# First weights ahead of the tokens, half-column token loads, idle transposes, and layer norm squares about the first half's mean

## The chip, the cores and the metric

The kernel runs on one core of one Trainium2 chip. The metric is the device time of one execution in microseconds (us), smaller being better; a kernel's time is the median of several runs. TensorE (PE) multiplies, VectorE (DVE), ScalarE (ACT) and GpSimd (POOL) do the elementwise work, and SyncE (SP) issues the transfers (DMA).

## The reference

A two-layer encoder trunk on 512 tokens of width 1024, all in float32. Each layer is three sub-layers, and each ends in a layer norm of a scaled residual plus the sub-layer's output:

```
def layer_norm(x, g, b):
    mu = jnp.mean(xf, axis=-1, keepdims=True)
    var = jnp.mean(jnp.square(xf - mu), axis=-1, keepdims=True)
    y = (xf - mu) * lax.rsqrt(var + LN_EPS)
    return y * g + b

def swiglu(x, w_gate, w_up, w_down):
    return (jax.nn.silu(x @ w_gate) * (x @ w_up)) @ w_down
...
x = layer_norm(ALPHA * x + 0.5 * swiglu(x, ...), ...)
x = layer_norm(ALPHA * x + mix, ...)      # attention and S5 in layer 0, pooling and gMLP in layer 1
x = layer_norm(ALPHA * x + 0.5 * swiglu(x, ...), ...)
```

So there are six layer norms, four feed-forward blocks (FFN, inner width 2816) and two mixers.

## The kernel before

Tokens lie in four tiles of 128 rows. For the matmuls, x is held transposed: `xh` and `xl` are [128, 8 blocks of columns, 512 tokens]. Every float32 product is three matmuls of reduced-precision parts: `split` (lines 88 to 96) copies the high part on ACT (line 91) and subtracts it on DVE for the low part (line 93), and `mm3` (lines 120 to 126) issues hi x hi, hi x lo, lo x hi. Weights come as 512 KB blocks `raw` (four buffers), are split into `whi` and `wlo`, and are used once. `to_xt` (line 128) turns one token tile: for each half `h` of its columns, four PE transposes into one PSUM bank, then a split into `xh` and `xl`; so a tile gives two xh copies on ACT and two xl subtractions on DVE.

The start: `load_x` (line 207) asks on SP's queue, in turn, for token tile 0, gate weights 0, tile 1, gate weights 1, tiles 2 and 3. Tiles 0 and 1 are turned and gate weights split in a fixed order on ACT and DVE (`as_written` chains the instructions of a block on an engine). Tiles 2 and 3 are left in `pending`. The first FFN (`ffn`, line 222) takes the weights in groups of 256 columns, gate (`m` = 0) and up (`m` = 1). The first group is worked in two halves of tokens: 48 matmuls of 256 tokens for the gate, then `flush`, which runs what is pending, 48 for the up weights, then the other 256 tokens of both. `cols` (line 201) runs over the eight column blocks `k`. Beside these matmuls DVE does `s5_prepare` (line 509), some hundreds of small instructions that make the S5 mixer's tables from one packed input, `s5pk`; it lies in the buffer of tiles 0 and 1, so its load waits until they are turned. On PE the order is the order of the code; on DVE and ACT the scheduler sets it, outside the blocks that `as_written` chains.

The layer norm: each of six blocks ends in `ln_tile` (line 153) or in the same steps, per token tile: two `add_to` on DVE add a bank of 512 columns to the residual `z` and give its sum, `ln_rest` (line 165) makes the negative mean `nmu`, ACT squares both halves about it and sums them (line 173), DVE makes (z - mean) g (line 176), POOL adds the two sums (line 177) and makes the reciprocal deviation `rs` in two steps (`rstd`, lines 142, 143), and DVE scales (line 185, or 182 for the last FFN, whose halves go out by DMA). The next `flush` turns the tile for the next block.

Of the kernel before, what the change touches and what calls it, by code (L numbers as in the profile page):

```python
# [16 lines left out]
P = 128  # L17
# [16 lines left out]
LATE = 3  # L34
NEG = -1e30
# [13 lines left out]
class Trunk:  # L49
# [3 lines left out]
    def __init__(self, ctx, tc):  # L53
# [14 lines left out]
        self.pending = []  # L68
# [4 lines left out]
    @contextmanager  # L73
    def as_written(self, *engines):

        ins = self.nc.cur_bb.bb.instructions
        last = ins[-1]
        yield
        start = next(k for k in reversed(range(len(ins))) if ins[k] is last) + 1
        info = mybir.DependencyInfo(mybir.DependencyClass.NoSync, mybir.DependencyReason.DATA)  # L80
        for e in engines:
            todo = [i for i in ins[start:] if i.engine == e]
            for a, b in zip(todo, todo[1:]):
                self.tc.add_manual_dep(b, a.name, info, reason="as_written")
# [22 lines left out]

    def halves(self, raw, shape):
        hi = self.w.tile([P] + shape, F32R, tag="whi", name="whi")
        lo = self.w.tile([P] + shape, F32R, tag="wlo", name="wlo")  # L110
# [17 lines left out]
    def to_xt(self, t, src):  # L128
        for h in range(2):
# [23 lines left out]
    def ln_tile(self, t, z, p0, p1, yscale, g, b, out=None, spill=None):  # L153

        s = self.sm.tile([P, 6], F32, name="st")
# [9 lines left out]
    def ln_rest(self, t, z, s, junk, g, b, out=None, spill=None):  # L165


        nc = self.nc
        nmu = s[:, 2:3]
        nc.vector.scalar_tensor_tensor(out=nmu, in0=s[:, 0:1], scalar=s[:, 1:2], in1=self.cst[:, 1:2],  # L170
                                       op0=ALU.add, op1=ALU.mult)
        for h, p in enumerate(junk):
            nc.scalar.activation(out=p, in_=z[:, h * 512:(h + 1) * 512], func=AF.Square, bias=nmu,  # L173
                                 accum_out=s[:, 3 + h:4 + h])
        n = self.w.tile([P, D], F32, tag="zf", name="zf", bufs=2)
        nc.vector.scalar_tensor_tensor(out=n, in0=z, scalar=nmu, in1=g, op0=ALU.add, op1=ALU.mult)
        nc.gpsimd.tensor_tensor(out=s[:, 5:6], in0=s[:, 3:4], in1=s[:, 4:5], op=ALU.add)  # L177
        rs = self.rstd(s[:, 5:6], 1.0 / D, EPS)
# [22 lines left out]
    def cols(self, bks, stat, a=0, b=SEQ):  # L201

        for k in range(NK):
            for bk, f in bks:
# [3 lines left out]
    def load_x(self, x, xt):  # L208

        raw = []  # L210
        for t in range(NT):
            self.nc.sync.dma_start(xt[t], x[t * P:(t + 1) * P])
            if t < 2:
                raw.append(self.fetch(*self.coming[t]))
        with self.as_written(mybir.EngineType.Activation, mybir.EngineType.DVE):
            for t in range(2):
                self.to_xt(t, xt[t])
                self.got.append(self.halves(raw[t], self.coming[t][1]))
# [4 lines left out]
    def ffn(self, xt, wg, wu, wd, g_ap, b_ap, out=None, spill=None, fetch=None, side=None, res=4):  # L223
        nc, tc = self.nc, self.tc
        with tc.tile_pool(name="act", bufs=1, reuse_waits="tile") as ap, \
# [5 lines left out]
            with self.as_written(*([mybir.EngineType.PE] if late else [])):  # L231
                for fg in range(NF // 2):
# [19 lines left out]
                    if jobs:  # L252
                        for m in range(2):
                            self.cols(*jobs[m], 0, 256)
                            self.flush(0 if late else 1 - m)
# [1021 lines left out]
def kernel(ctx, tc, x, ln_g, ln_b, wg, wu, wd, ab_in, ab_out, rel, s5pk, w_glu,  # L1277
# [8 lines left out]
    with tc.tile_pool(name="xa", bufs=1, reuse_waits="tile") as xa:  # L1286
# [13 lines left out]
        first(wg[0, 0], 0, 256)  # L1300
        k.load_x(x, x_tiles())
# [62 lines left out]
```

## Time and profile before

| | |
|---|---|
| median of 3 runs | 1817.14 us (1815.19 to 1817.96) |
| the profiled execution | 1817.25 us, its span 1815.5 us |
| PE busy | 1786.5 us (98%), 8752 matmuls and transposes |
| DVE, ACT, POOL busy | 1104.4 (61%), 690.4 (38%), 32.1 us (2%) |
| DMA | 212.77 MB, 117 GB/s on average |
| mean granted PE clock | 0.998 |

The span runs from the first to the last instruction; the execution's time holds 1.75 us more. A row of a timeline gives start, length, engine, line, operation, output and inputs, and, in brackets, how long the engine stood idle before it and what ended that. Matmuls are pipelined, so the distance of two starts tells their cost, not the length of one.

### The profile page before, as it was taken

The page shows a single profiled execution, that of the slowest core. Times are in us where ns is not written, and L with a number is a line of the kernel's source. Part 1 is how long each engine was busy: PE and PEld are TensorE (multiplying, and loading weights), DVE is VectorE, ACT ScalarE, POOL GpSimd, SP SyncE. Part 2 cuts the span into 40 slices and gives each one's busy share as a digit, 9 for nine tenths or more (in the row PEclk, how much of TensorE's full clock was granted, in tenths as well). Part 3 has the DMA queues.
Part 4 walks back from the last instruction along what each step waited for, and adds up shares of the span by engine and source line. Part 5 has one row for each costly group of instructions (what it writes and reads, how often), then busy time and mean ns, then how long its engine had stood idle before and what let it go on. Part 6 is the DMA issues. An engine that isn't in the chain of part 4 may idle for free.

```text
span 1815.5 us, 22309 instructions
## 1 busy us (share of the span) xinstructions
PE 1786.5 (98%) x8752; PEld 1497.6 (82%) x8752; DVE 1104.4 (61%) x1783; ACT 690.4 (38%) x983; POOL 32.1 (2%) x119
## 2 busy tenths in 40 slices
PE   8999999999999999999999999999999999999998
PEld 7888888888887888888888888888878898888886
DVE  7866542266766657658436585574488566747635
ACT  4233431245767433333324333332264343333322
POOL 0000000010000100000000000000010000000000
PEclk9999999999999999999999999999999999999999
DMA  6335633255422551532334324223333152531321
GB/s 207 107 116 168 203 105 104 94 163 166 128 94 73 177 194 47 177 102 67 112 99 139 107 89 142 82 81 116 117 98 105 58 186 68 153 104 58 123 97 58
DMA packets 168377, 212.77 MB, mean 117 GB/s; under 512 B 7888, under 2 KB 130000, under 8 KB 168272
## 3 DMA queue, kind: packets, MB, share of 16 engines
q1 hardware_dynamic: 168272, 211.35, 37.0%
q8 instruction: 68, 1.11, 0.3%
q14 instruction: 37, 0.30, 0.1%
HBM read 196.12 MB, written 14.16 MB: 116 GB/s over the span
## 4 chain that ended last, share of the span: by engine, by line
issue 60%; PE 33%; DVE 3%; ACT 1%; DMA 1%; POOL 1%; POOLq 0%; SPq 0%; DVEq 0%; ACTq 0%
PE ps L124 10%; PE ps L125 10%; PE ps L126 10%; PE ps L810 1%; DVE wlo L93 1%; POOL rs L143 1%; DMA s5tl<-side 1%; PE ps L858 0%; PE ps L850 0%; PE ps L133 0%; DMA x<-in_x_dram 0%; DVE pl L93 0%; PE ps L849 0%; ACT ps L173 0%; POOL st L177 0%
## 5 line engine op out<-in xcount | busy, mean ns | idle before, releaser
L124 PE MATMUL ps<-xh,whi 128*128 128x512 f32 (+1 forms) x1696 | 639.0, 377 | 0.8 <-ACT xh L91 0.8
L125 PE MATMUL ps<-xl,whi 128*128 128x512 f32 (+1 forms) x1696 | 635.0, 374 | 4.0 <-DVE xl L93 4.0
L126 PE MATMUL ps<-xh,wlo 128*128 128x512 f32 (+1 forms) x1696 | 634.4, 374 | 0.0
L93 DVE TENSOR_TENSOR wlo<-raw,whi 128x1024 fp32r<-128x1024 f32 x313 | 381.7, 1221 | 337.5 <-ACT whi L91 334.9
L91 ACT ACTIVATE whi<-raw 128x1024 fp32r<-128x1024 f32 x313 | 330.3, 1058 | 655.1 <-PE ps L125 370.3
L124 PEld LDWEIGHTS ps<-xh,whi 128*128 128x128 f32 x1696 | 320.6, 189 | 59.8 <-issue 3.1
L125 PEld LDWEIGHTS ps<-xl,whi 128*128 128x128 f32 x1696 | 320.6, 189 | 59.4 <-DVE xl L93 5.2
L126 PEld LDWEIGHTS ps<-xh,wlo 128*128 128x128 f32 x1696 | 320.5, 189 | 56.7
L124 PE MATMUL ps<-whi,sl 128*128 128x512 f32 x480 | 187.2, 390 | 0.0
L126 PE MATMUL ps<-whi,sl 128*128 128x512 f32 x480 | 186.9, 389 | 0.0
L125 PE MATMUL ps<-wlo,sl 128*128 128x512 f32 x480 | 186.9, 389 | 0.0
L126 PEld LDWEIGHTS ps<-whi,sl 128*128 128x128 f32 x480 | 90.2, 188 | 18.7
L125 PEld LDWEIGHTS ps<-wlo,sl 128*128 128x128 f32 x480 | 90.2, 188 | 18.5
L124 PEld LDWEIGHTS ps<-whi,sl 128*128 128x128 f32 x480 | 90.2, 188 | 18.4
L162 DVE SCALAR_TENSOR_TENSOR xb<-ps,xb 128x512 f32<-128x512 f32 x128 | 83.0, 683 | 23.5 <-PE ps L126 23.4
L334 DVE SCALAR_TENSOR_TENSOR th<-th,ps 128x512 f32<-128x512 f32 x66 | 44.9, 684 | 73.5 <-ACT th L333 73.0
L333 ACT ACTIVATE th<-ps 128x512 f32<-128x512 f32 x66 | 38.8, 592 | 121.4 <-PE ps L126 121.4
L93 DVE TENSOR_TENSOR sl<-hb,sl 128x1792 fp32r<-128x1792 f32 x24 | 48.6, 2023 | 31.9 <-ACT sl L91 31.9
L341 DVE TENSOR_TENSOR hb<-th,ps 128x512 f32<-128x512 f32 x48 | 32.6, 687 | 56.0 <-PE ps L126 56.0
L91 ACT ACTIVATE sl<-hb 128x1792 fp32r<-128x1792 f32 x24 | 40.8, 1700 | 44.6 <-DVE hb L348 44.6
L91 ACT ACTIVATE whi<-b 128x1024 fp32r<-128x1024 f32 x36 | 38.1, 1059 | 39.6 <-PE ps L126 38.2
L93 DVE TENSOR_TENSOR wlo<-b,whi 128x1024 fp32r<-128x1024 f32 x36 | 44.0, 1221 | 14.2 <-ACT whi L91 14.2
(327 smaller groups left out, 1905.2 us busy)
## 6 DMA issues: line engine op xcount, KB each, us to landing
raw<-in_wg_dram SPq DMA_DIRECT2D x88, 512.0 KB, 3.6
raw<-in_wu_dram SPq DMA_DIRECT2D x88, 512.0 KB, 3.6
raw<-in_wd_dram SPq DMA_DIRECT2D x76, 512.0 KB, 3.3
b<-in_wd_dram SPq DMA_DIRECT2D x24, 512.0 KB, 5.4
raw<-in_ab_in_dram SPq DMA_DIRECT2D x20, 512.0 KB, 4.4
raw<-in_cd_in_dram SPq DMA_DIRECT2D x12, 512.0 KB, 3.7
x<-in_x_dram SPq DMA_DIRECT2D x8, 512.0 KB, 7.1
s<-zf SPq DMA_DIRECT2D x8, 512.0 KB, 4.5
```

The source lines that it names most:

```text
L91: nc.scalar.activation(out=hi, in_=src, func=AF.Copy, scale=scale)
L93: nc.vector.tensor_tensor(out=lo, in0=src, in1=hi.bitcast(F32), op=ALU.subtract)
L124: mm(ps, ah, bh, start=start, stop=False)
L125: mm(ps, ah, bl, start=False, stop=False)
L126: mm(ps, al, bh, start=False, stop=stop)
L143: nc.gpsimd.tensor_tensor(out=v[:, 1:2], in0=v[:, 0:1], in1=self.cst[:, 0:1], op=ALU.pow)
L162: self.nc.vector.scalar_tensor_tensor(out=zz, in0=p, scalar=scale, in1=zz, op0=ALU.mult, op1=ALU.add, **({} if total is None else {"accum_ ...
L333: nc.scalar.activation(out=th, in_=bk[0, f], func=AF.Tanh, scale=0.5)
L334: nc.vector.scalar_tensor_tensor(out=th, in0=th, scalar=1.0, in1=bk[0, f], op0=ALU.add, op1=ALU.mult)
L341: tt(out=hb[:, 0::7] if f == 0 else hb[:, 1:3], in0=th.rearrange("p (a c) -> p a c", a=2), in1=bk[1, f].rearrange("p (a c) -> p a c", a=2) ...
L810: nc.tensor.matmul(banks[h][:, o:o + w], a[r, i * P:i * P + P], b[r, :w], start=n == 0, stop=n == 2)
```

## The change

Four things. The queue: gate weights 0, the first 512 columns of tiles 0 and 1, gate weights 1, their other columns, tile 2, both up weights, tile 3. PE: 20 transposes of the identity into a bank that nobody reads, then only the first halves of tiles 0 and 1; the second halves follow in the middle of the gate's first 48 matmuls (`mid`). Tile 3 is turned after the up weights' 48 matmuls, not beside tile 2 (`flush(1 - m)`). The layer norm: `c`, the mean of the first 512 columns, is made on POOL after the first `add_to`; both squares are taken about `c`, the first before the second half is added; POOL corrects the variance by (mean - c) squared, seven small instructions in place of three.

```diff
+WARM = 20
...
-        self.pending = []
+        self.pending, self.mid = [], []
     @contextmanager
-    def as_written(self, *engines):
+    def as_written(self, *engines, after=()):
         ins = self.nc.cur_bb.bb.instructions
         last = ins[-1]
...
         start = next(k for k in reversed(range(len(ins))) if ins[k] is last) + 1
         info = mybir.DependencyInfo(mybir.DependencyClass.NoSync, mybir.DependencyReason.DATA)
         for e in engines:
-            todo = [i for i in ins[start:] if i.engine == e]
+            todo = [i for i in after if i.engine == e] + [i for i in ins[start:] if i.engine == e]
             for a, b in zip(todo, todo[1:]):
                 self.tc.add_manual_dep(b, a.name, info, reason="as_written")
...
         self.nc.sync.dma_start(raw, ap)
         return raw
+    def hi_lo(self, shape):
+        return [self.w.tile([P] + shape, F32R, tag=n, name=n) for n in ("whi", "wlo")]
     def halves(self, raw, shape):
-        hi = self.w.tile([P] + shape, F32R, tag="whi", name="whi")
-        lo = self.w.tile([P] + shape, F32R, tag="wlo", name="wlo")
+        hi, lo = self.hi_lo(shape)
         self.split(raw, hi, lo)
         return hi, lo
...
         mm(ps, ah, bl, start=False, stop=False)
         mm(ps, al, bh, start=False, stop=stop)
-    def to_xt(self, t, src):
-        for h in range(2):
+    def to_xt(self, t, src, hs=(0, 1)):
+        for h in hs:
             p = self.bank()
             for j in range(4):
                 k = 4 * h + j
...
     def ln_tile(self, t, z, p0, p1, yscale, g, b, out=None, spill=None):
-        s = self.sm.tile([P, 6], F32, name="st")
+        s = self.sm.tile([P, 8], F32, name="st")
         for h, p in enumerate((p0, p1)):
             self.add_to(z[:, h * 512:(h + 1) * 512], p, yscale, s[:, h:h + 1])
         self.ln_rest(t, z, s, (p0, p1), g, b, out, spill)
...
     def ln_rest(self, t, z, s, junk, g, b, out=None, spill=None):
         nc = self.nc
-        nmu = s[:, 2:3]
+        nmu, c, q = s[:, 2:3], s[:, 5:6], s[:, 6:8]
+        ts = nc.gpsimd.tensor_scalar
+        ts(out=c, in0=s[:, 0:1], scalar1=-2.0 / D, scalar2=None, op0=ALU.mult)
+        for h, p in enumerate(junk):
+            nc.scalar.activation(out=p, in_=z[:, h * 512:(h + 1) * 512], func=AF.Square, bias=c,
+                                 accum_out=s[:, 3 + h:4 + h])
         nc.vector.scalar_tensor_tensor(out=nmu, in0=s[:, 0:1], scalar=s[:, 1:2], in1=self.cst[:, 1:2],
                                        op0=ALU.add, op1=ALU.mult)
-        for h, p in enumerate(junk):
-            nc.scalar.activation(out=p, in_=z[:, h * 512:(h + 1) * 512], func=AF.Square, bias=nmu,
-                                 accum_out=s[:, 3 + h:4 + h])
         n = self.w.tile([P, D], F32, tag="zf", name="zf", bufs=2)
         nc.vector.scalar_tensor_tensor(out=n, in0=z, scalar=nmu, in1=g, op0=ALU.add, op1=ALU.mult)
-        nc.gpsimd.tensor_tensor(out=s[:, 5:6], in0=s[:, 3:4], in1=s[:, 4:5], op=ALU.add)
-        rs = self.rstd(s[:, 5:6], 1.0 / D, EPS)
+        nc.gpsimd.tensor_tensor(out=q[:, 0:1], in0=nmu, in1=c, op=ALU.subtract)
+        nc.gpsimd.tensor_tensor(out=q[:, 0:1], in0=q[:, 0:1], in1=q[:, 0:1], op=ALU.mult)
+        ts(out=q[:, 1:2], in0=s[:, 3:4], scalar1=1.0 / D, scalar2=EPS, op0=ALU.mult, op1=ALU.add)
+        nc.gpsimd.tensor_tensor(out=q[:, 1:2], in0=q[:, 1:2], in1=q[:, 0:1], op=ALU.subtract)
+        rs = self.rstd(s[:, 4:5], 1.0 / D, q[:, 1:2])
         if out is not None:
             for h in range(2):
                 c = slice(h * 512, h * 512 + 512)
...
     def cols(self, bks, stat, a=0, b=SEQ):
         for k in range(NK):
+            if k == NK // 2 and self.mid:
+                self.mid.pop()()
             for bk, f in bks:
                 hi, lo = stat(k, f)
                 self.mm3(bk[:, a:b], hi, lo, self.xh[:, k, a:b], self.xl[:, k, a:b], k == 0, k == NK - 1)
     def load_x(self, x, xt):
+        w, sync = self.coming, self.nc.sync.dma_start
+        def ask(t, h):
+            c = slice(512 * h, 512 * h + 512)
+            sync(xt[t][:, c], x[t * P:(t + 1) * P, c])
         raw = []
-        for t in range(NT):
-            self.nc.sync.dma_start(xt[t], x[t * P:(t + 1) * P])
-            if t < 2:
-                raw.append(self.fetch(*self.coming[t]))
-        with self.as_written(mybir.EngineType.Activation, mybir.EngineType.DVE):
+        for h in range(2):
+            raw.append(self.fetch(*w[h]))
+            ask(0, h)
+            ask(1, h)
+        sync(xt[2], x[2 * P:3 * P])
+        raw += [self.fetch(*a) for a in w[2:4]]
+        sync(xt[3], x[3 * P:4 * P])
+        bk = self.bank()
+        for i in range(WARM):
+            self.nc.tensor.transpose(bk[:, 0:P], self.ident, self.ident)
+        order = mybir.EngineType.Activation, mybir.EngineType.DVE
+        self.got = [self.hi_lo(w[i][1]) for i in range(4)]
+        with self.as_written(*order):
+            self.split(raw[0], *self.got[0])
             for t in range(2):
-                self.to_xt(t, xt[t])
-                self.got.append(self.halves(raw[t], self.coming[t][1]))
+                self.to_xt(t, xt[t], (0,))
+        ins = self.nc.cur_bb.bb.instructions
+        last = [next(i for i in reversed(ins) if i.engine == e) for e in order]
+        got = list(self.got)
+        def rest():
+            with self.as_written(*order, after=last):
+                self.split(raw[1], *got[1])
+                for t in range(2):
+                    self.to_xt(t, xt[t], (1,))
+                for i in (2, 3):
+                    self.split(raw[i], *got[i])
+        self.mid = [rest]
         for t in range(2, NT):
             self.pending.append(lambda t=t: self.to_xt(t, xt[t]))
...
                     if jobs:
                         for m in range(2):
                             self.cols(*jobs[m], 0, 256)
-                            self.flush(0 if late else 1 - m)
+                            self.flush(1 - m)
                         for m in range(2):
                             self.cols(*jobs[m], 256, SEQ)
                     for f in range(2):
...
         def side(slots):
             return k.s5_prepare(s5pk, [xa.tile([P, 2048], F32, tag=f"x{i}", name=f"xs{i}") for i in range(2)] + slots)
         first(wg[0, 0], 0, 256)
+        both = k.coming
+        first(wu[0, 0], 0, 256)
+        k.coming = both + k.coming
         k.load_x(x, x_tiles())
         first(ab_in, 2 * AW, 256)
         k.ffn(None, wg[0, 0], wu[0, 0], wd[0, 0], ln_g[0, 0], ln_b[0, 0], spill=s0, side=side, fetch=x_again)```

How this moves instructions. SP's queue at the start, before (`raw` of `in_wg` are gate weights, of `in_wu` up weights):

```order
L212 DMA x0_93<-in_x_dram 128x1024
L105 DMA raw_96<-in_wg_dram 128x4x256
L212 DMA x0_93<-in_x_dram 128x1024
L105 DMA raw_99<-in_wg_dram 128x4x256
L212 DMA x1_94<-in_x_dram 128x1024 x2
L105 DMA raw_165<-in_wu_dram 128x4x256
L105 DMA raw_171<-in_wu_dram 128x4x256
L535 DMA xs0_412<-in_s5pk_dram 128x1090
```

and with the change:

```order
L106 DMA raw_95<-in_wg_dram 128x4x256
L226 DMA x0_93<-in_x_dram 128x512 x2
L106 DMA raw_99<-in_wg_dram 128x4x256
L226 DMA x0_93<-in_x_dram 128x512 x2
L232 DMA x1_94<-in_x_dram 128x1024
L106 DMA raw_104<-in_wu_dram 128x4x256
L106 DMA raw_106<-in_wu_dram 128x4x256
L234 DMA x1_94<-in_x_dram 128x1024
L106 DMA raw_439<-in_wg_dram 128x4x256
L106 DMA raw_445<-in_wg_dram 128x4x256
L572 DMA xs0_435<-in_s5pk_dram 128x1090
```

Besides the new order of tokens and weights, `s5pk` now stands behind the two gate blocks of the second group (`raw_439`, `raw_445`).

DVE's order from the load of `s5pk` on, before (`bglu` is its first reader; `ps_225` to `ps_246` are the banks of token tiles 2 and 3; the rows on 128x16 tiles are `s5_prepare`):

```order
L540 TENSOR_SCALAR bglu_551<-xs0_412 128x2
L496 TENSOR_SCALAR xs0_412<-xs0_412 128x16
...
L505 TENSOR_SCALAR xs0_412<-xs0_412 128x16
L503 SCALAR_TENSOR_TENSOR xs0_412<-xs0_412 128x16 x4
L93 TENSOR_TENSOR xl_70<-ps_225,xh_69 128x4x128
L93 TENSOR_TENSOR xl_70<-ps_232,xh_69 128x4x128
L93 TENSOR_TENSOR xl_70<-ps_239,xh_69 128x4x128
L93 TENSOR_TENSOR xl_70<-ps_246,xh_69 128x4x128
L503 SCALAR_TENSOR_TENSOR xs0_412<-xs0_412 128x16
```

and with the change (`ps_248`, `ps_255` are tile 2, `ps_310`, `ps_317` tile 3):

```order
L577 TENSOR_SCALAR bglu_574<-xs0_435 128x2
L533 TENSOR_SCALAR xs0_435<-xs0_435 128x16
...
L94 TENSOR_TENSOR xl_70<-ps_248,xh_69 128x4x128
L94 TENSOR_TENSOR xl_70<-ps_255,xh_69 128x4x128
L536 SCALAR_TENSOR_TENSOR xs0_435<-xs0_435 128x16
...
L614 SCALAR_TENSOR_TENSOR xs0_435<-xs0_435 128x16
L615 TENSOR_SCALAR xs0_435<-xs0_435 128x16
L94 TENSOR_TENSOR xl_70<-ps_310,xh_69 128x4x128
L94 TENSOR_TENSOR xl_70<-ps_317,xh_69 128x4x128
```

Tile 3's two rows have moved behind 54 instructions of `s5_prepare`, counted from L536 to L615. Ahead of `bglu`, DVE's order is now: the split of gate block 0, the first halves of tiles 0 and 1, gate block 1, their second halves, the copy that waits for POOL, and three weight splits.

## Rows read from the trace of the kernel before

**Rows 1.** The page's busy shares.
```profile
PE 1786.5 (98%) x8752; PEld 1497.6 (82%) x8752; DVE 1104.4 (61%) x1783; ACT 690.4 (38%) x983; POOL 32.1 (2%) x119
```

**Rows 2.** The timeline of 0 to 22 us: start, length, engine, instruction, count, idle before.
```profile
1.50 0.28 POOL masks.py:199 TENSOR_SCALAR_AFFINE_SELECT ident<-ident 128x128 f32<-128x128 f32 x1
...
4.47 1.94 PE L133 MATMUL ps<-ident,x 128*128 128x128 f32 x8 [4.47 <-DMA x<-in_x_dram]
...
7.99 1.97 PE L133 MATMUL ps<-ident,x 128*128 128x128 f32 x8 [1.58 <-DMA x<-in_x_dram]
...
10.48 0.18 DVE L614 COPY xs<-xs 128x16 f32<-128x16 f32 x1 [2.73 <-POOL xs L592]
...
12.45 0.58 PE L125 MATMUL ps<-xl,whi 128*128 128x256 f32 x1 [2.08 <-DVE xl L93]
...
19.85 1.91 PE L133 MATMUL ps<-ident,x 128*128 128x128 f32 x16
...
21.52 0.36 PE L124 MATMUL ps<-xh,whi 128*128 128x256 f32 x1
```

**Rows 3.** Busy time by stretch: length, engines (instructions), granted clock, DMA share, GB/s.
```profile
12.40:16.10 3.70, 3.65 (x17) 3.65 (x18) 3.39 (x4) 2.12 (x2) 0.00 (x0) 1.00 1.05 383
...
16.10:19.70 3.60, 3.60 (x31) 3.60 (x31) 2.82 (x9) 1.06 (x1) 0.00 (x0) 1.00 0.98 316
```

**Rows 4.** The timeline of SyncE's queue and the DMA issues at 9.98 (us to landing).
```profile
9.98 0.34 SPq L535 DMA_DIRECT2D xs<-in_s5pk_dram  x1
...
xs<-in_s5pk_dram SPq DMA_DIRECT2D x1, 545.0 KB, 5.9
```

**Rows 5.** DVE's timeline from 19 to 29 us.
```profile
19.86 0.81 DVE L503 SCALAR_TENSOR_TENSOR xs<-xs 128x16 f32<-128x16 f32 x4
...
21.12 2.48 DVE L93 TENSOR_TENSOR xl<-ps,xh 128x512 fp32r<-128x512 f32 x4 [0.45 <-ACT xh L91]
...
24.75 0.17 DVE L557 TENSOR_TENSOR xs<-xs 128x16 f32<-128x16 f32 x1
...
28.46 0.17 DVE L578 TENSOR_SCALAR xs<-xs 128x16 f32<-128x16 f32 x1
```

**Rows 6.** Timelines of DVE and PE at four stage borders.
```profile
393.60 1.28 DVE L185 SCALAR_TENSOR_TENSOR zf<-zf,rs,lnb 128x1024 f32<-128x1024 f32 x1 [1.25 <-POOL rs L143]
...
396.08 0.39 PE L125 MATMUL ps<-wlo,xh 128*128 128x256 f32 x1 [0.82 <-DVE wlo L93]
...
619.89 1.28 DVE L185 SCALAR_TENSOR_TENSOR zf<-zf,rs,lnb 128x1024 f32<-128x1024 f32 x1 [0.99 <-POOL rs L143]
...
621.83 0.39 PE L125 MATMUL ps<-xl,whi 128*128 128x256 f32 x1 [0.88 <-DVE xl L93]
...
634.19 1.03 PE L133 MATMUL ps<-ident,zf 128*128 128x128 f32 x8
...
636.20 0.39 PE L125 MATMUL ps<-xl,whi 128*128 128x256 f32 x1 [0.34 <-DVE xl L93]
...
1335.97 1.64 DVE L185 SCALAR_TENSOR_TENSOR zf<-zf,rs,lnb 128x1024 f32<-128x1024 f32 x1 [1.51 <-POOL rs L143]
...
1340.81 0.73 PE L124 MATMUL ps<-whi,xh 128*128 128x512 f32 x2 [1.42 <-ACT whi L91]
```

**Rows 7.** Busy time by stretch around 566 us, columns as in rows 3.
```profile
562.10:565.50 3.40, 2.14 (x10) 1.39 (x10) 3.33 (x7) 2.35 (x4) 0.00 (x0) 1.00 0.44 148
...
566.00:569.00 3.00, 3.00 (x17) 2.39 (x15) 2.92 (x9) 0.98 (x2) 0.00 (x0) 0.50 0.50 158
```

**Rows 8.** The timeline of the last layer norm, from 1807.9 us.
```profile
1807.99 0.22 DVE L170 SCALAR_TENSOR_TENSOR st<-st,cst 128x1 f32<-128x1 f32 x1
...
1808.31 0.69 ACT L173 ACTIVATE ps<-xb,st 128x512 f32<-128x512 f32 x1 [3.92 <-DVE st L170]
...
1809.91 0.19 POOL L177 TENSOR_TENSOR st<-st 128x1 f32<-128x1 f32 x1 [4.34 <-ACT ps L173]
...
1811.04 1.41 DVE L182 SCALAR_TENSOR_TENSOR zf<-zf,rs,lnb 128x512 f32<-128x512 f32 x2 [1.51 <-POOL rs L143]
```

## The prediction

> **What bounds the kernel now.** I read four views in this order: the busy shares, the timeline of the first 22 us, the waits of TensorE (PE) with the rows around each, and the timeline of the tail. PE is busy for 98% of the span [rows 1], so a change that leaves the matmul count alone can win only what PE loses outside them. That happens in three places. First, the start: PE does the transposes of token tiles 0 and 1 as their 512 KB land (from 4.47 and 7.99), then one matmul, and stands until 12.45 for xl [rows 2]. xl was late because VectorE (DVE) sat until 10.48 on a small copy that waits for GpSimd (POOL); the splits stand behind that copy. From 12.4 to 16.1 PE then starts 17 matmuls of 256 columns, 0.218 us each, the 1.2 GHz level; from 16.1 to 19.7 it starts 31, 0.116 us each, the 2.4 GHz level [rows 3]. The granted-clock column prints 1.00 for both, so here the pitch tells it. Second, the stage borders, where PE waits a little behind a layer norm. Third, the tail, where the last layer norm runs with PE done.
>
> **Loads.** The changed queue brings gate weights and half columns first. Before, the first block of 512 KB was there at 4.47 [rows 2] and s5pk, the ninth in the queue, at 9.98 + 5.9 = 15.9 [rows 4]: (15.9 - 4.47) / 8 = 1.4 us a block. The first megabyte in the new order is block wg 0 plus the halves of tiles 0 and 1. The first block took until 4.47 and the third until 7.99, so I take 6.2 for two (ends 5.7 and 7.0).
>
> **PE's path, if nothing else binds.** ident is ready at 1.78 [rows 2]. Eight transposes took 1.94 in the low clock, about 0.21 each, so the twenty idle ones end near 6.0, about when the data are there: they cost nothing. The eight real ones follow, two xh copies and two xl copies of about 0.62 (from [rows 5]: four took 2.48), and matmuls run from 8.5. With the clock up, 23 x 0.12 = 2.8 brings 11.3. There the second halves begin: eight transposes 0.95, then xh and xl of the second tile, matmuls again at 13.85 (a stop of about 1.6 us that the old order did not have), 23 more until 16.6. Before, that point was 19.85 [rows 2]: 3.2 us won. Tile 2's eight transposes bring 17.55, the 48 matmuls of the up weights 23.3, and now tile 3's transposes come directly ahead of the matmuls that need them. Such a place costs 2.0 us from the transposes to the matmul on xl (634.19 to 636.20) [rows 6], so 25.3. Before, this point was 21.52 + 48 x 0.12 = 27.3. Won on PE's path alone: 2.0 us.
>
> **DVE's path, which I take to bind.** In the changed order, xl of tile 3 stands behind 54 small instructions on 128x16 tiles; before, all four xl of tiles 2 and 3 stood right behind the first few. All of these wait for s5pk, and s5pk is now asked for behind two more weight blocks: 15.9 + 2 x 1.4 = 18.7. Its issue still waits for the transposes of tiles 0 and 1 (now at about 12.2, before 9.98), which costs nothing as the queue is full until then. Then four small ones (0.2 each, as the serial row of [rows 5]: four in 0.81) give 19.45, two xl of tile 2 20.7. Of the 54, the 41 from L557 to L578 of the old line numbers took 24.75 to 28.57 = 3.8; the other 13 are eleven serial ones at 0.2 and two at 0.1, 2.45. Together 6.25: xl of tile 3 starts at 26.95, and PE goes on at 27.6. Against 27.3 the start is **0.3 us slower**: the win is won and given back. Bounds: -2.0 (PE's path alone) to +4.9 (below). What DVE does afterwards is late as well; PE next needs it for the weights of the following group, 96 matmuls of 0.12 later, and that covers it.
>
> **The clock in that stop.** PE would stand from about 24.6 to 27.6 behind a microsecond of transposes. The trace has one fall of the clock: after a stretch in which PE was busy 2.14 of 3.4 us, the granted clock was 0.50 from 566 to 569 [rows 7]. The new stop is emptier, so I count a fall: 3 us at half speed cost **1.5**. Bounds 0 and 1.7.
>
> **Tail.** Now the last tile's mean is formed at 1807.99, two squares follow, three POOL instructions, and the last scaling starts at 1811.04 [rows 8]. After: the first half's square is done before; the second starts at about 1808.0, and takes 0.69 + 0.19. POOL meanwhile needs the mean (1808.21), then five dependent instructions: four at 0.27 and the power at 0.55 (three took 1.13, [rows 8]), which ends near 1809.9. Won: **1.1** (ends 0 and 1.4). The two POOL instructions that don't need the mean lie beside other work.
>
> **Borders.** At three of them a scaling that waits for POOL's rs is ahead of what PE waits for [rows 6]. At 393.60 DVE had idled 1.25 for rs, the weight split came behind it, and PE waited 0.82 at 396.08: with rs 1.1 earlier, 0.8 goes. At 619.89 (0.99 idle) xl follows and PE waited 0.88; but ScalarE (ACT) now has an extra square of tile 3 ahead of the weight copy, which moves the split back: I take 0.4. At 1335.97 (1.51 idle) ACT's copies follow, and PE waited 1.42 at 1340.81; DVE's mean now stands behind one more weight split: 0.6. Sum **1.8** (ends 0 and 2.8). The stops from transposes to xl (634.19) have no layer norm in them and stay.
>
> **Sum.** 1817.25 (the profiled execution's own time; the median is 0.11 lower) + 0.3 + 1.5 - 1.1 - 1.8 = **1816.15**; I give 1816.2.
>
> **Rivals.**
> A. *DVE's line does not bind* (s5pk lands sooner, or the small instructions pass faster). For it: the old order let PE run straight through. Against: 54 instructions are counted, and their rows are there. Start -2.0, no stop, so no fall: 1817.25 - 2.0 - 2.9 = 1812.4, faster.
> B. *The idle transposes do not raise the clock.* The trace tells neither: sixteen transposes between 4.47 and 9.96, with a gap, left the clock low, but PE stood 2.1 us after them. Then 23 matmuls from 9.15 at 0.218 end at 14.2, the second halves' stop (with transposes at 0.24) at 17.4, the next 23 at 22.4, tile 2's transposes at 24.3. This decides from the moment tile 2's xh is later than 19.45: DVE stands at tile 2's xl, the 54 wait too, and every microsecond goes through. xl of tile 2 ends at 25.3, 54 more 31.55, PE goes on at 32.2: +4.9 at the start. With the 2.9 of the layer norms 1819.25, slower than before by 2; without them 1822. If the clock rises in the middle of the first 23, it is about +1. The Trainium skill (TensorE: Matmul & The Clock Gate, Part 4: PE-mode transpose) says that the full clock does not engage for transposes, which don't count as PE work in the same way. By that rule B holds and the sum is 1819; no run here shows it for a stretch of transposes alone.
> C. *The layer norm's gain is not there*: POOL has seven instructions for three, and DVE's order at the borders moves other things back by as much. 1817.25 + 0.3 + 1.5 = 1819.05.
>
> **How the numbers follow.** Forecast 0.40, A 0.15, B 0.30, C 0.15. I take 0.2% (3.6 us) as what a measurement can tell from no change. Below 1813.5 lie A and a little of the forecast with all ends good: 0.18. Above 1820.8 lies B with a small layer norm gain: 0.10. The rest, 0.72, is the same. The range runs from A's 1812.4 to B with most of its price, 1820.0.
>
> **What would show it.** Right: matmul pitch 0.12 from the first real matmul; a wait of PE for xl of 2 to 3 us ending near 27.6, with DVE's small instructions ahead of it; the last scaling about 2 us behind the start of the last mean, not 3; PE's waits at the first and third border gone or halved. Wrong: no wait near 25 to 27 (A); pitch 0.21 until 12 or later, and that wait ending past 28 (B); the last scaling still 3 us behind the mean (C).

## The result and the profile after

The changed kernel takes 1828.06 us (median of 4 runs, 1827.15 to 1828.82) against 1816.16 us for the kernel before (4 runs, 1814.32 to 1817.96): ratio 1.0063, interval 1.0051 to 1.0075. It is **slower by 11.9 us**. I had forecast 1816.2 us and no difference that can be measured, so the forecast was wrong, and the time lies outside its range. The profiled execution spans 1825.4 us (before 1815.5), 9.9 us more. Of the runs below, one execution of best_a (3002.56 us) and one of best_b (1977.50 us) had a mean granted clock of 0.56 and 0.85, and the ratios leave them out. Where TensorE (PE) falls behind, read from the starts of the same instructions in both timelines:

| Point of the program (start in the kernel before) | PE behind the kernel before, us |
|---|---|
| 149.4 | 1.0 |
| behind the first layer norm (397.0) | 0.0 |
| ahead of the stop at 562.8 | 1.5 |
| behind it (578.5) | 2.7 |
| behind the second layer norm (634.2) | 3.4 |
| behind the third (988.3) | 4.9 |
| at the fourth (1338.5) | 7.2 |
| PE's last matmul (1806.8) | 7.8 |
| end of the span | 9.9 |

The start costs one microsecond, but it doesn't reach the end: at 388 us the kernel before waits longer for the low part of a weight than the changed one, and behind that the two are level (PE's timelines, the kernel before and then the changed one):

```profile
388.39 0.39 PE L125 MATMUL ps<-wlo,xh 128*128 128x256 f32 x1 [1.57 <-DVE wlo L93]
388.41 0.39 PE L128 MATMUL ps<-wlo,xh 128*128 128x256 f32 x1 [0.99 <-DVE wlo L94]
```

Of the 9.9 us, about 1.4 come back in the first mixer (attention and S5, 397 to 563), 1.2 at the stop behind it, where the clock falls, 5.1 at the borders of the later layer norms, and 2.1 in the tail. The page's busy shares of the changed kernel, as in [rows 1]:

```profile
PE 1791.4 (98%) x8772; PEld 1499.0 (82%) x8772; DVE 1103.6 (60%) x1783; ACT 690.4 (38%) x983; POOL 79.3 (4%) x215
```

GpSimd (POOL) has 96 instructions more and is busy 47 us longer, half a microsecond for each, where [rows 8] had 0.19 for such a row. That is the first thing to look into.

**The start** of the changed kernel, its timeline from 0 to 29 us (answers [rows 2, 5]):

```profile
1.84 4.53 PE L237 MATMUL ps<-ident 128*128 128x128 f32 x20 [1.84 <-POOL ident masks.py:199]
...
6.16 1.12 PE L136 MATMUL ps<-ident,x 128*128 128x128 f32 x8
...
8.85 0.38 PE L128 MATMUL ps<-xl,whi 128*128 128x256 f32 x1 [0.45 <-DVE xl L94]
...
14.32 0.39 PE L128 MATMUL ps<-xl,whi 128*128 128x256 f32 x1 [0.45 <-DVE xl L94]
...
19.52 0.17 DVE L577 TENSOR_SCALAR bglu<-xs 128x2 f32<-128x2 f32 x1 [0.41 <-DMA xs<-in_s5pk_dram]
...
27.51 0.17 DVE L615 TENSOR_SCALAR xs<-xs 128x16 f32<-128x16 f32 x1
27.59 1.29 DVE L94 TENSOR_TENSOR xl<-ps,xh 128x512 fp32r<-128x512 f32 x2
28.33 0.39 PE L128 MATMUL ps<-xl,whi 128*128 128x256 f32 x1 [2.87 <-DVE xl L94]
```

It goes as forecast, step by step some 0.3 to 0.8 us later: matmuls at 8.85 (8.5), again at 14.32 (13.85), `s5pk` at 19.5 (18.7), tile 3's xl behind the small instructions at 27.59 (26.95), PE on at 28.33 (27.6). The twenty idle transposes took 0.23 us each; the eight behind them took 0.14.

**The clock.** The busy time by stretch in the changed kernel, columns as in [rows 3, 7]:

```profile
10.00:11.70 1.70, 1.70 (x16) 1.70 (x15) 1.22 (x1) 0.00 (x0) 0.00 (x0) 1.00 1.06 383
...
25.00:28.30 3.30, 0.38 (x1) 0.19 (x1) 3.30 (x33) 0.52 (x2) 0.00 (x0) 1.00 0.01 2
28.30:31.50 3.20, 3.17 (x26) 3.17 (x27) 3.10 (x26) 0.23 (x1) 0.00 (x0) 1.00 0.00 0
...
565.50:569.00 3.50, 2.59 (x16) 2.12 (x16) 3.47 (x6) 1.22 (x2) 0.00 (x0) 0.59 0.06 15
569.00:572.00 3.00, 3.00 (x10) 1.89 (x8) 2.11 (x10) 1.74 (x7) 0.00 (x0) 0.50 0.43 161
572.00:576.00 4.00, 4.00 (x21) 2.66 (x21) 1.50 (x7) 2.73 (x11) 0.00 (x0) 0.88 0.00 0
```

The first matmuls start 0.11 to 0.12 us apart (16 in 1.70 us; the 2.4 GHz level, where [rows 3] had 0.218). In this execution the clock did not fall in the stop at 25 to 28. Behind 566 it stayed low for longer than in [rows 7]: 0.41 x 3.5 + 0.50 x 3 + 0.12 x 4 = 3.4 us of work lost, if PE had been busy throughout. The same two stretches of the kernel before:

```profile
565.50:569.00 3.50, 3.50 (x20) 2.82 (x18) 3.42 (x9) 1.22 (x2) 0.00 (x0) 0.54 0.43 136
569.00:572.00 3.00, 3.00 (x17) 1.84 (x15) 1.92 (x10) 2.56 (x11) 0.00 (x0) 0.97 0.05 19
```

There it was 0.46 x 3.5 + 0.03 x 3 = 1.7, so the change loses up to 1.7 us more; PE falls behind by 1.2 there (table).

**Borders**, timelines of VectorE (DVE) and PE in the changed kernel; the rows at 393 to 396, 625 and 1348 answer [rows 6]:

```profile
393.21 1.28 DVE L194 SCALAR_TENSOR_TENSOR zf<-zf,rs,lnb 128x1024 f32<-128x1024 f32 x1 [1.66 <-POOL rs L146]
396.11 0.39 PE L128 MATMUL ps<-wlo,xh 128*128 128x256 f32 x1 [0.82 <-DVE wlo L94]
...
625.20 0.39 PE L128 MATMUL ps<-xl,whi 128*128 128x256 f32 x1 [1.59 <-DVE xl L94]
...
978.24 1.28 DVE L194 SCALAR_TENSOR_TENSOR zf<-zf,rs,lnb 128x1024 f32<-128x1024 f32 x1 [1.66 <-POOL rs L146]
979.45 0.68 DVE L165 SCALAR_TENSOR_TENSOR xb<-ps,xb 128x512 f32<-128x512 f32 x1
980.79 0.39 PE L128 MATMUL ps<-xl,whi 128*128 128x256 f32 x1 [1.24 <-DVE xl L94]
...
1337.27 0.50 PE L127 MATMUL ps<-whi,xh 128*128 128x512 f32 x1 [0.88 <-ACT whi L92]
1338.53 0.50 PE L128 MATMUL ps<-wlo,xh 128*128 128x512 f32 x1 [0.76 <-DVE wlo L94]
1348.17 0.73 PE L127 MATMUL ps<-whi,xh 128*128 128x512 f32 x2 [1.60 <-ACT whi L92]
```

DVE now idles 1.66 us for rs ahead of a scaling, and the wait at 396 stayed at 0.82. The wait on xl at the next border grew from 0.88 to 1.59, and three waits are new (980.79, 1337.27, 1338.53). DVE's instruction groups, of the kernel before and then of the changed one, give the sum (idle time ahead of the group in the last columns):

```profile
L185 DVE SCALAR_TENSOR_TENSOR zf<-zf,rs,lnb 128x1024 f32<-128x1024 f32 x20 | 26.0, 1302 | 17.7 <-POOL rs L143 17.7
```

```profile
L194 DVE SCALAR_TENSOR_TENSOR zf<-zf,rs,lnb 128x1024 f32<-128x1024 f32 x20 | 26.0, 1302 | 30.7 <-POOL rs L146 30.7
```

**The tail** of the changed kernel, the timeline of the last layer norm (answers [rows 8]):

```profile
1816.91 0.68 DVE L165 SCALAR_TENSOR_TENSOR xb<-ps,xb 128x512 f32<-128x512 f32 x1
1817.08 0.22 POOL L175 TENSOR_SCALAR st<-st 128x1 f32<-128x1 f32 x1 [2.14 <-DVE xb L165]
1817.64 0.22 DVE L179 SCALAR_TENSOR_TENSOR st<-st,cst 128x1 f32<-128x1 f32 x1
1817.90 1.28 DVE L182 SCALAR_TENSOR_TENSOR zf<-xb,st,lng 128x1024 f32<-128x1024 f32 x1
1818.23 1.00 POOL L185 TENSOR_SCALAR st<-st 128x1 f32<-128x1 f32 x1 [0.93 <-ACT ps L177]
1819.31 0.19 POOL L183 TENSOR_TENSOR st<-st 128x1 f32<-128x1 f32 x1
...
1820.51 0.57 POOL L146 TENSOR_TENSOR rs<-rs,cst 128x1 f32<-128x1 f32 x1
1821.11 1.41 DVE L191 SCALAR_TENSOR_TENSOR zf<-zf,rs,lnb 128x512 f32<-128x512 f32 x2 [1.93 <-POOL rs L146]
```

From the last mean to the last scaling it is now 3.47 us; before it was 3.05, and I had expected 2. A POOL instruction of 0.19 (L185) takes 1.00 and ends at 1819.23, just behind DVE's 128x1024 instruction (1817.90 + 1.28 = 1819.18); four small ones and the power follow one by one.

**What holds POOL.** Three pairs from the changed kernel's timeline show it:

```profile
390.27 1.28 DVE L182 SCALAR_TENSOR_TENSOR zf<-x,st,lng 128x1024 f32<-128x1024 f32 x1
390.38 1.22 POOL L183 TENSOR_TENSOR st<-st 128x1 f32<-128x1 f32 x1 [3.69 <-DVE st L179]
...
619.32 0.19 POOL L183 TENSOR_TENSOR st<-st 128x1 f32<-128x1 f32 x1 [0.64 <-DVE st L179]
619.33 1.28 DVE L182 SCALAR_TENSOR_TENSOR zf<-z,st,lng 128x1024 f32<-128x1024 f32 x1
...
621.21 1.22 DVE L94 TENSOR_TENSOR wlo<-raw,whi 128x1024 fp32r<-128x1024 f32 x1 [0.59 <-ACT whi L92]
621.32 1.25 POOL L145 TENSOR_SCALAR rs<-st 128x1 f32<-128x1 f32 x1
```

The same instruction (L183) takes 0.19 when it starts a moment ahead of DVE's and 1.22 when it starts behind it, and it then ends 0.05 us after DVE's does. Of its 24 rows, the 13 that start 0.05 us or more inside DVE's instruction take 1.22 to 1.29, the other eleven 0.19. So it is with the weight split (L94), another DVE instruction that reads two tensors from SBUF. The add that reads one of its two from PSUM holds nothing: L175 took 0.22 inside it (1817.08, above). The Trainium skill (SBUF — State Buffer, SBUF: two separate sides) says just that: DVE with two SBUF inputs and a GpSimd instruction that reads SBUF share one pair of ports, whoever is first has it for the whole instruction, and the other waits. These rows agree for POOL as the one that waits; that DVE waits they don't show, as it took its 1.28 at 619.33 too. The old layer norm kept clear of it in 22 of its 24 adds (the other two took 0.49 and 0.75): in the tail its POOL add came at 1809.91 [rows 8], behind the end of DVE's instruction, as both squares had to end first.

### The profile page after: what moved, and what is told of

Same layout as the page of the kernel before. It is cut to its first block, busy times and chain, and to the rows that moved or that the text cites. A ratio compares the mean times of both kernels' runs of the same rounds, so it can differ in the third digit from the quotient of the medians.

```text
span 1825.4 us, 22447 instructions
## 1 busy us (share of the span) xinstructions
PE 1791.4 (98%) x8772; PEld 1499.0 (82%) x8772; DVE 1103.6 (60%) x1783; ACT 690.4 (38%) x983; POOL 79.3 (4%) x215
## 4 chain that ended last, share of the span: by engine, by line
PE 88%; DVE 5%; ACT 2%; POOL 2%; issue 1%; DMA 1%; POOLq 0%; DVEq 0%; SPq 0%; ACTq 0%
PE ps L128 29%; PE ps L127 29%; PE ps L129 29%; DVE wlo L94 1%; PE ps L847 1%; DVE xl L94 1%; PE ps L136 1%; POOL st L183 0%; DVE zf L194 0%; ACT whi L92 0%; ACT pr L857 0%; DVE pl L94 0%; DMA xs<-in_s5pk_dram 0%; POOL rs L146 0%; PE ps L895 0%
## 5 line engine op out<-in xcount | busy, mean ns | idle before, releaser
L128 PE MATMUL ps<-xl,whi 128*128 128x512 f32 (+1 forms) x1696 | 633.9, 374 | 7.8 <-DVE xl L94 7.8
L127 PE MATMUL ps<-xh,whi 128*128 128x512 f32 (+1 forms) x1696 | 637.8, 376 | 2.5 <-ACT xh L92 2.5
L94 DVE TENSOR_TENSOR wlo<-raw,whi 128x1024 fp32r<-128x1024 f32 x313 | 381.5, 1221 | 345.8 <-ACT whi L92 343.8
L92 ACT ACTIVATE whi<-raw 128x1024 fp32r<-128x1024 f32 x313 | 330.2, 1058 | 650.9 <-PE ps L128 373.5
L128 PEld LDWEIGHTS ps<-xl,whi 128*128 128x128 f32 x1696 | 319.4, 188 | 64.4 <-DVE xl L94 9.9
L127 PEld LDWEIGHTS ps<-xh,whi 128*128 128x128 f32 x1696 | 319.3, 188 | 62.2 <-ACT xh L92 3.9
L127 PE MATMUL ps<-whi,sl 128*128 128x512 f32 x480 | 187.1, 390 | 0.0
L128 PE MATMUL ps<-wlo,sl 128*128 128x512 f32 x480 | 186.7, 389 | 0.0
L128 PEld LDWEIGHTS ps<-wlo,sl 128*128 128x128 f32 x480 | 90.1, 188 | 18.6
L127 PEld LDWEIGHTS ps<-whi,sl 128*128 128x128 f32 x480 | 90.1, 188 | 18.5
L165 DVE SCALAR_TENSOR_TENSOR xb<-ps,xb 128x512 f32<-128x512 f32 x128 | 82.5, 682 | 17.4 <-PE ps L129 17.4
L175 POOL TENSOR_SCALAR st<-st 128x1 f32<-128x1 f32 x24 | 5.3, 222 | 1633.7 <-DVE xb L165 1065.9
L94 DVE TENSOR_TENSOR sl<-hb,sl 128x1792 fp32r<-128x1792 f32 x24 | 48.6, 2023 | 31.8 <-ACT sl L92 31.8
L92 ACT ACTIVATE sl<-hb 128x1792 fp32r<-128x1792 f32 x24 | 40.8, 1699 | 44.5 <-DVE hb L385 44.5
L92 ACT ACTIVATE whi<-b 128x1024 fp32r<-128x1024 f32 x36 | 38.1, 1059 | 39.7 <-PE ps L129 38.2
```

Source lines behind the costliest of these rows:

```text
L92: nc.scalar.activation(out=hi, in_=src, func=AF.Copy, scale=scale)
L94: nc.vector.tensor_tensor(out=lo, in0=src, in1=hi.bitcast(F32), op=ALU.subtract)
L127: mm(ps, ah, bh, start=start, stop=False)
L128: mm(ps, ah, bl, start=False, stop=False)
L165: self.nc.vector.scalar_tensor_tensor(out=zz, in0=p, scalar=scale, in1=zz, op0=ALU.mult, op1=ALU.add, **({} if total is None else {"accum_ ...
L175: ts(out=c, in0=s[:, 0:1], scalar1=-2.0 / D, scalar2=None, op0=ALU.mult)
```

## Experiments

Two theories of the layer norm stood at the beginning. **P**: rs is late, as POOL is held and then has five instructions in a row. **O**: DVE's changed order costs. In the tail and at the borders of 966 and 1320 us of the old kernel, the add of the next tile's first half stood ahead of the scaling; now it stands behind it, so a scaling that waits for rs holds up the add too. The third layer norm in the kernel before (DVE's timeline; the changed kernel's rows at 978.24 and 979.45 are above):

```profile
972.50 0.69 DVE L162 SCALAR_TENSOR_TENSOR xb<-ps,xb 128x512 f32<-128x512 f32 x1 [0.45 <-PE ps L126]
...
973.56 1.28 DVE L185 SCALAR_TENSOR_TENSOR zf<-zf,rs,lnb 128x1024 f32<-128x1024 f32 x1 [0.36 <-POOL rs L143]
```

All ratios are to the kernel before, run on the same chip in turn.

| Run | us, median | ratio, interval |
|---|---|---|
| start_only | 1818.24 | 1.0008, 1.0000 to 1.0017 |
| ln_only | 1824.06 | 1.0042, 1.0029 to 1.0055 |
| ln_act_corr | 1826.67 | 1.0058, 1.0045 to 1.0071 |
| ln_order | 1818.23 | 1.0009, 1.0000 to 1.0018 |
| ln_act_corr8 | 1816.52 | 0.9998, 0.9989 to 1.0007 |
| b_st9 | 1827.55 | 1.0058, 1.0044 to 1.0072 |
| start_flush0 | 1813.62 | 0.9980, 0.9971 to 0.9989 |
| start_cold | 1819.13 | 1.0011, 1.0002 to 1.0019 |
| after_flush0 | 1822.26 | 1.0029, 1.0017 to 1.0041 |
| flush0_cold | 1815.74 | 0.9993, 0.9984 to 1.0002 |
| best_b | 1813.88 | 0.9979, 0.9970 to 0.9988 |
| best_a | 1812.07 | 0.9976, 0.9967 to 0.9985 |

The kernel before had medians of 1816.69, 1816.72 and 1817.08 us beside the first, second and third four of them in time.

**start_only and ln_only: the two halves of the change.** The one is the changed kernel with the old `ln_rest`, the other the old kernel with the new one:

```diff
 # start_only
-        ts(out=c, in0=s[:, 0:1], scalar1=-2.0 / D, scalar2=None, op0=ALU.mult)
...
+        rs = self.rstd(s[:, 5:6], 1.0 / D, EPS)
 # ln_only
+        ts(out=c, in0=s[:, 0:1], scalar1=-2.0 / D, scalar2=None, op0=ALU.mult)
...
+        rs = self.rstd(s[:, 4:5], 1.0 / D, q[:, 1:2])
```

> The changed start (weights first, half columns, idle transposes, one token tile turned per group of matmuls) with the old layer norm. Theory S (the lag between the two traces is 1.0 us after the start and grows only at layer norms): 1816.2 + 1.0 = 1817.2 us, and the clock is low once for about 3.4 us near 566 as before. Rival (the start moves later things, as the second low stretch of the clock near 570): 1819 us or more. My forecast on record had +1.8 for this part, 1818.

> The old start with the changed layer norm. Theory L (the layer norm is the loss: rs comes later after the mean, not sooner): 1816.2 + 9 to 11 = 1825 to 1827 us, the last scaling starts 3.4 to 3.5 us behind the start of the last mean, as in the changed kernel. Rival (start and layer norm only lose together, through their different phase): under 1820 us. My forecast on record had -2.9 for this part, 1813.3.

Measured: +1.5 and +7.4 us. The layer norm is most of the loss, as theory L had it (1824 against 1825 to 1827, a little less; the last scaling comes 3.46 us behind the mean). start_only lies between theory S (1817.2) and its rival (1819). The two sum to 8.9 where the change cost 11.9; this is taken up below. In start_only's profiled execution the clock did fall behind the stop of 25 to 28 us:

```profile
28.30:31.50 3.20, 3.20 (x17) 3.20 (x17) 3.10 (x29) 0.00 (x0) 0.00 (x0) 0.50 0.00 0
```

**ln_act_corr: the correction on ScalarE.** As ln_only, but:

```diff
-        nc.gpsimd.tensor_tensor(out=q[:, 0:1], in0=nmu, in1=c, op=ALU.subtract)
-        nc.gpsimd.tensor_tensor(out=q[:, 0:1], in0=q[:, 0:1], in1=q[:, 0:1], op=ALU.mult)
-        ts(out=q[:, 1:2], in0=s[:, 3:4], scalar1=1.0 / D, scalar2=EPS, op0=ALU.mult, op1=ALU.add)
-        nc.gpsimd.tensor_tensor(out=q[:, 1:2], in0=q[:, 1:2], in1=q[:, 0:1], op=ALU.subtract)
+        ts(out=q[:, 0:1], in0=s[:, 3:4], scalar1=1.0 / D, scalar2=EPS, op0=ALU.mult, op1=ALU.add)
+        nc.scalar.activation(out=s[:, 8:9], in_=c, func=AF.Square, scale=-1.0, bias=nmu)
+        nc.scalar.activation(out=q[:, 1:2], in_=s[:, 8:9], func=AF.Identity, scale=-1.0, bias=q[:, 0:1])
```

and the scratch tile `st` made 9 words wide for the new column. 

> As ln_only, but the correction of the squares is worked out by ScalarE (two instructions on 128x1 behind the second square) and one early GpSimd instruction, so that behind the mean GpSimd has only the scale and the power. Theory P (a GpSimd instruction that meets VectorE's 128x1024 instruction is held until that ends, and four more GpSimd instructions follow it one by one): the scale is ready about when the 128x1024 instruction ends, the last scaling starts 2.4 to 2.7 us behind the mean (3.05 in the kernel before, 3.47 in the changed one), and the time falls to 1815 to 1818 us. Rival O (VectorE's changed order is what costs, the scaling standing ahead of the next tile's first add): that order stays as in the changed kernel, so the time stays at 1822 us or more.

Measured: 1826.67 us, by its time a win for O. But PE's waits for xl had gone down (4.2 us for 6.1 in ln_only), and the loss lay where no layer norm is: in each feed-forward block PE took 2.6 us more (638.4 to 972.8, before 634.2 to 966.0) with no wait. The run said nothing on P or O until that was explained.

**ln_order: the old order of DVE.** As ln_only, with the scaling kept back until the next tile's first add:

```diff
-        nc.vector.scalar_tensor_tensor(out=n, in0=n, scalar=rs, in1=b, op0=ALU.mult, op1=ALU.add)
...
+        if spill is None and t < NT - 1:
+            self.later = scale
+        else:
+            scale()
 # ln_tile
-            self.add_to(z[:, h * 512:(h + 1) * 512], p, yscale, s[:, h:h + 1])
+            with self.as_written(*([mybir.EngineType.DVE] if h == 0 and self.later else [])):
+                self.add_to(z[:, h * 512:(h + 1) * 512], p, yscale, s[:, h:h + 1])
+                if h == 0 and self.later:
+                    self.later()
+                    self.later = None
```

> As ln_only, but in the layer norms that write no copy for a later reload (two borders, the last one and others of the same kind) the scaling of a tile is put behind the first add of the next tile on VectorE, as the kernel before has it. Rival O (the order costs): 1817 to 1819 us, within 3 us of the kernel before. Theory P (the late rs costs, order is second): the last layer norm gets back about 1.9 us and the borders with that order about as much each at most, rs itself still comes 3.4 us behind the mean, and the time is 1820 to 1823 us.

Measured: 1818.23, 5.8 us less than ln_only, where O had it and P (1820 to 1823) did not. rs still came 3.2 us behind the mean; the DVE instruction ahead of it now uses the time (ln_order's timeline near the end):

```profile
1805.60 0.69 DVE L167 SCALAR_TENSOR_TENSOR xb<-ps,xb 128x512 f32<-128x512 f32 x1 [0.45 <-PE ps L127]
...
1806.81 1.41 DVE L194 SCALAR_TENSOR_TENSOR zf<-zf,rs,lnb 128x512 f32<-128x512 f32 x2 [0.51 <-POOL rs L144]
```

**ln_act_corr8 and b_st9: the confound taken out.** ln_act_corr with its new column put into one that is free by then and the scratch tile back at 8 words, and the kernel before with a wider scratch tile and nothing else:

```diff
 # ln_act_corr8
+        nc.scalar.activation(out=s[:, 0:1], in_=c, func=AF.Square, scale=-1.0, bias=nmu)
 # b_st9
-        s = self.sm.tile([P, 6], F32, name="st")
+        s = self.sm.tile([P, 9], F32, name="st")
```

> ln_act_corr again, with the scratch tile of the layer norm 8 words wide (32 bytes a partition, as in the changed kernel) where it had 9 (36 bytes). In ln_act_corr the matmuls that read the activation tiles behind that tile took 6 ns more each than in every other kernel. Theory P (the late rs is the root, VectorE's order only does harm because rs is late): with that gone 1815 to 1818 us, 10 us below ln_act_corr, with VectorE's order as in the changed kernel. Rival O (the order costs by itself): 1821 us or more.

> The kernel before, with nothing changed but the scratch tile of the layer norm: 9 words a partition for 6, so that every buffer allocated behind it moves. Theory A (where the buffers lie sets the pace of the matmuls that read them): four feed-forward blocks each 2.6 us longer, 1816.5 + 10.5 = 1827 us, no wait on TensorE changed. Rival (ln_act_corr was slow by its two ScalarE instructions): 1816 to 1817 us.

Both came out as A and P had them. b_st9 is 10.8 us slower than the kernel before by three more words of scratch. The matmuls that read the `sl` tiles take 6 ns more each (so do those on `act`, which the first feed-forward block has in their place); those on xh and xl, allocated ahead of the scratch tile, do not (groups of PE from 640 to 960 us, the kernel before and then b_st9):

```profile
L124 PE MATMUL ps<-xh,whi 128*128 128x512 f32 x320 | 124.6, 389 | 0.0
...
L124 PE MATMUL ps<-whi,sl 128*128 128x512 f32 x140 | 54.5, 389 | 0.0
```

```profile
L124 PE MATMUL ps<-xh,whi 128*128 128x512 f32 x320 | 124.5, 389 | 0.0
L124 PE MATMUL ps<-whi,sl 128*128 128x512 f32 x134 | 52.9, 395 | 0.0
```

ln_act_corr8, with DVE's order as in ln_only, is back at the kernel before. DVE's idle time ahead of its scalings fell from 38.0 us in ln_only to 21.3 (20.3 in the kernel before). In the tail rs gained less: the last scaling is 2.97 us behind the mean, not the 2.4 to 2.7 that P had. So neither P nor O holds alone: **either a rs that comes in time or an order that doesn't stand behind it takes nearly the whole loss away** (1816.5 and 1818.2 against 1824.1). The loss is their product.

**start_flush0: the four xl together again.** As start_only, but:

```diff
-                            self.flush(1 - m)
+                            self.flush(0 if late else 1 - m)
```

> As start_only, but tiles 2 and 3 are both turned behind the first group of matmuls, as in the kernel before, so that VectorE's four xl instructions stand ahead of most of the 54 small ones. Theory D (VectorE's line, with the small instructions ahead of tile 3's xl, binds the start): the wait of 2 to 3 us at 25 to 28 goes and with it the fall of the clock, TensorE is about 2 us ahead of the kernel before from there on, 1814 to 1815 us. Rival (the loads bind: tile 3 or the packed constants land too late for it): the wait only moves, 1817 us or more.

Measured: 1813.62, just below theory D's 1814 to 1815 and 4.6 us below start_only. PE has no stop there any more (start_flush0's timeline, and its busy time by stretch):

```profile
20.16 2.48 DVE L94 TENSOR_TENSOR xl<-ps,xh 128x512 fp32r<-128x512 f32 x4
```

```profile
25.00:28.30 3.30, 3.30 (x30) 3.30 (x29) 3.23 (x35) 0.30 (x1) 0.00 (x0) 1.00 0.01 2
```

**start_cold and flush0_cold: no idle transposes.** As start_only and as start_flush0, with

```diff
-WARM = 20
+WARM = 0
```

> As start_only, without the twenty idle transposes. Theory W (transposes alone raise the clock): without them the eight real ones take 0.21 to 0.24 us each and the first matmuls start 0.21 to 0.22 us apart until about 10 to 12 us; TensorE reaches tile 2's transposes some 2 us later, and as VectorE's line has about 1 us of slack there, the time is 0.5 to 1.5 us above start_only, 1818.7 to 1819.8. Rival B of the prediction (transposes don't count for the clock): pitch and time as in start_only, within 0.3 us.

> start_flush0 without the twenty idle transposes. With VectorE's line out of the way the slower start of TensorE should go through whole: 2 us, 1815.5 to 1816 us. Rival (the loads of tiles 2 and 3 or the packed constants bind there, so that idle transposes buy nothing): 1813.6 as start_flush0.

Measured: 1819.13, 0.9 us above start_only (the intervals overlap), and 1815.74, 2.1 above start_flush0 (the intervals just meet). In start_cold the first matmuls are slow (busy time by stretch, start_cold and then start_flush0):

```profile
9.50:12.00 2.50, 2.50 (x13) 2.50 (x13) 1.22 (x1) 0.06 (x1) 0.00 (x0) 1.00 1.07 386
```

```profile
9.50:12.00 2.50, 2.50 (x23) 2.50 (x23) 1.23 (x1) 0.55 (x1) 0.00 (x0) 1.00 1.05 382
```

So the idle transposes do raise the clock. Their 2 us go through to the end only where DVE's line does not bind, as far as these intervals tell; in the profiled executions PE is 1.8 us further ahead at 149 us with them (start_flush0 against flush0_cold).

**after_flush0, best_b, best_a: towards a better kernel.** The changed kernel with start_flush0's line; that with ln_act_corr8's correction; that with ln_order's order.

```diff
 # after_flush0, best_b, best_a
+                            self.flush(0 if late else 1 - m)
 # best_b, best_a
+        nc.scalar.activation(out=s[:, 0:1], in_=c, func=AF.Square, scale=-1.0, bias=nmu)
...
 # best_a
+            self.later = scale
```

> The changed kernel with one line put back: tiles 2 and 3 are both turned behind the first group of matmuls. Theory D: the same 4 to 5 us come off as between start_only and start_flush0, 1828 - 4.6 = 1823 to 1824 us, and no wait near 25 to 28. Rival (the parts interact): under 1821 or over 1826 us.

> after_flush0 with ScalarE working out the correction, as in ln_act_corr8. Theories D and P together: 1813.6 (start_flush0) - 0.2 (ln_act_corr8 against before) = 1813 to 1814 us, 14 us below the changed kernel. If the layer norm's rest of the change is worth anything by now, under 1813.

> As best_b, and in the layer norms that write no copy the scaling of a tile is put behind the first add of the next tile, as in ln_order. Theory: the last tile's first square is then done before the mean, the last scaling starts 2.4 to 2.5 us behind the mean (3.05 in the kernel before), 0.6 us less in the tail and up to 1 us at two borders: 1812 to 1813 us. Rival (rs is early enough, so the order no longer matters): as best_b.

Measured: 1822.26 (5.8 below the changed kernel, a microsecond more than expected), 1813.88 and 1812.07 us. best_a and best_b beat both kernels; their intervals overlap, so the order is not shown to matter once rs is in time. In best_a the last scaling starts 2.44 us behind the mean (its timeline):

```profile
1809.29 0.22 DVE L184 SCALAR_TENSOR_TENSOR st<-st,cst 128x1 f32<-128x1 f32 x1
...
1811.73 1.41 DVE L196 SCALAR_TENSOR_TENSOR zf<-zf,rs,lnb 128x512 f32<-128x512 f32 x2 [0.90 <-POOL rs L147]
```

That saves 0.6 us of the tail, yet neither is shown to be faster than start_flush0, which has the old layer norm. The new layer norm is worth nothing that these runs can tell.

## Why the prediction was wrong

- **The start, +0.3, and the clock, +1.5: near enough where they were forecast, and luck at the end.** At 149 us PE was 1.0 behind in the changed kernel, without the fall of the clock, and 2.1 in start_only's profiled execution, with it. But the wait of 1.57 us that the kernel before has at 388.39, which the prediction left out, took up the lag in both: they are 0.04 behind at 397. The +1.5 that start_only measured (+0.8 in its profiled execution) stems from the first mixer, where PE falls behind by 0.9 again; why was not tried. DVE's line binds (rival A fell): its one line put back gave 4.6 us. The forecast of PE's path alone was -2.0; start_flush0 gave -3.1 (-2.3 at 149 us). Of the clock's fall behind the stop the two profiled executions show one of each kind, so the 1.5 is a term that some executions pay. How many do was not measured.
- **Rival B fell.** The pitch was 0.11 to 0.12 from the first block of matmuls on. The rule of the Trainium skill (TensorE: Matmul & The Clock Gate, Part 4: PE-mode transpose) that the full clock does not engage for transposes does not hold in these traces: PE ran nothing but transposes up to 8.0 us.
- **The tail, -1.1: the step that failed is "five dependent instructions: four at 0.27 and the power at 0.55".** The 0.27 came from rows in which POOL ran while DVE was idle [rows 8]. Behind the mean DVE runs 1.28 us on two SBUF tensors, and the POOL instruction that meets it takes 1.0 to 1.2. The sentence after it failed too: the two instructions that don't need the mean do not lie beside other work when one of them (L185) is itself held, ahead of the others in POOL's queue. Measured: 3.47 us from mean to scaling, for 2. Between PE's end and the end of the span the tail gave +2.1 us, for -1.1.
- **The borders, -1.8: followed from that.** With rs later, DVE idles longer for it, 30.7 us for 17.7, and the borders from the second on gave +5.1. Of DVE's order there I had counted one more weight split ahead of the mean, not what the scaling would hold up. At the two borders where the next tile's add had stood ahead of the scaling, it now stood behind; there PE's new waits arose (980.79, 1337.27, 1338.53), and in the tail the last adds came late: the last mean starts 3.0 us behind PE's last matmul, before 1.2.
- **Rival C had the mechanism half**: POOL's count and DVE's order. Its sign came, the last scaling still 3 us behind the mean, but it priced them at nothing gained, 1819.05, and not at a loss. I had given the layer norm no bound on the slower side.
- **What stays open.** The halves cost 1.5 + 7.4 us, together 11.9. In the profiled executions it is 0.8 + 6.8 against 9.9. Of those 2.3 us, 1.3 arise in the stop near 566, with the longer stretch of half clock that neither half's profile has, and 1.0 ahead of it. The record points to more half clock in every execution: the mean granted clock of the whole span was 0.995 or 0.996 in all four of the changed kernel, 0.997 or 0.998 in all five of ln_only, and 0.995 to 0.998 in start_only's eleven. Why the two together bring it about was not tried.

## What to carry to other kernels

Price a small GpSimd instruction by what VectorE does at that moment: 0.19 to 0.23 us beside nothing or beside an instruction that reads PSUM, up to 1.3 behind one that reads two SBUF tensors (2.23 at 628.54 in the changed kernel, behind two in a row), and a chain of them starts only when that ends. When a chain is rebuilt, compare the order of work on every engine that waits for its result: work that had filled the wait may now stand behind it. And change one buffer's size only together with a look at the pace of the matmuls that read the buffers behind it.

## What was not expected of the hardware

- Twelve bytes more a partition in a scratch tile (four buffers of it) cost 10.8 us of 1817: 395 for 389 ns on each matmul that reads the `sl` and `act` tiles allocated behind it. 32 bytes, as in the change, did no harm. That it is where the buffers lie is inferred from the edit, which changes nothing else; their addresses were not read.
- The clock stayed at its full level through 3.3 us in which PE was busy 0.38 (25.00 to 28.30 in the changed kernel) and fell to half behind start_only's like stop, in which PE was busy 0.99.
- Twenty transposes on an idle chip were enough to bring the 2.4 GHz level to the eight behind them (0.14 for 0.21 to 0.24 us each) and to the first matmuls. They don't always do: in best_a's profiled execution (1817.78 us, where its median is 1812.07) four of the eight had to wait 1.90 us for their tokens, and behind that wait the granted clock was 0.50 from 9 to 15 us.
